# Start addresses of the large on-chip tiles moved to multiples of 512 bytes in an fp32 encoder layer

## The chip, the cores and the metric

The kernel runs on one core of one Trainium2 chip. The metric is the device time of one execution in microseconds (us). The kernel before took 1539.32 us (median of three runs, 1538.78 to 1539.38).

## The reference

One layer of an encoder over 1024 tokens of width 1024, all in float32, batch 1:

```
mod = silu(c) @ w_ada + b_ada                      -> sh1, sc1, gt1, sh2, sc2, gt2
h   = rms_norm(x, g_norm1) * (1 + sc1) + sh1
proj = h @ w_in                                    -> 8 heads of neighbourhood attention (qa, ka, va),
                                                      12 heads of dilated attention (qb, kb, vb), 2 x 1024 gates
o_a = softmax over an 8 x 16 window of a 16 x 64 grid, with a relative bias
o_b = three groups of 4 heads, dilations 1, 4, 16, merged by their log-denominators
merged = sigmoid(gate_a) * (o_a @ w_proj_a) + sigmoid(gate_b) * (o_b @ w_proj_b)
x   = x + gt1 * (merged @ w_o)
h2  = rms_norm(x, g_norm2) * (1 + sc2) + sh2
a, up = split(h2 @ w_ffn_in)                       (2 x 2816 columns)
x   = x + gt2 * ((silu(a) * up) @ w_ffn_out)
```

## The kernel before

**Precision.** Each large product is made of three matmuls. A float32 operand is split into `hi`, its rounding to the type `float32r`, and `lo = x - hi`, and the sum hi·hi + hi·lo + lo·hi is accumulated in PSUM (`PASS`, line 127). ScalarE makes `hi` (line 108), VectorE or GpSimd makes `lo` (line 109). A matmul has a stationary operand of 128 columns, loaded for it alone, and a moving operand of up to 512 columns, read from SBUF while it runs. Transposes, the row sums of line 263 and the product of probabilities and values (line 487) are plain float32.

**Stages**, in order of time in the profiled execution:

- 0 to 50 us: norm of x, modulation columns, the first unit's projection (lines 681 to 726).
- 50 to 600 us: ten units of two heads each. For each block of 128 tokens the projection (line 297: moving operand = weight tile `whi`/`wlo`, 384 columns; stationary = `hT`), transposes (355), scores (446), softmax, transposes of the probabilities (472), product with the values (487). Some gate products (604) follow at the end.
- 600 to 700 us: gate products by a scheme with seven instead of eight block products (623: moving = `hT` or the mixed blocks `tg`).
- 700 to 760 us: the two branch projections and the merge (995: moving = `oT`).
- 760 to 830 us: the output projection (1136: moving = kept weights `wr`, or `whi`/`wlo`).
- 830 to 1335 us: the first feed-forward product (1200: moving = `h2T`, or mixed blocks `t`; stationary = weights), again with seven products.
- 1335 to 1536 us: the second feed-forward product (1372: both operands are `whi`/`wlo` tiles), whose mixed weights `m` are loaded and formed at its start (lines 1343 to 1352).

**Order.** PE's order is the program's own (`manual_schedule`). Inside the first region the order of all engines is the program's; elsewhere a planner orders the other engines and the DMA queue by its own estimate. Nearly all DMAs are issued from SP.

**Where tiles lie.** SBUF is filled by two stacks of pools per partition, one growing up from the bottom (`left`), one growing down from the top (`right`). In a pool, tags are laid out in the order in which they are first allocated; each buffer is rounded up to 32 bytes. A pool that is opened after another was released lies on the same bytes, and a tile there waits for the last use of the tiles it covers (`reuse_waits="tile"`). At the very bottom lie 1024 bytes of DMA scratch and four constants of 32 bytes each. In the compiled program the starts of the large tiles, as remainders of 512 bytes, are:

| tiles | side | start mod 512 |
|---|---|---|
| `whi`, `wlo` (weight slots), `hT`, `h2T` (both parts), the `hi` halves of `tg`, `oT`, `t`, the tiles of the last stage `c11`.. and `x2` | left | 320 |
| the `lo` halves of `tg`, `oT`, `t`; `sg`, `wr`, `e`, `c`, `m`, `raw` | right | 480 |
| `yT`, `qk`, `land` and all of tag `big`, `PT`, `bmask`, `acc2` | right | 352 |
| `P`, `xd`, `stg` | right | 416 |
| `ident` | left | 448 |
| `xt` of the output projection, `tm`, `qn`, `rtab`, `gt1`, `sc2`, `sh2` | right | 0 |

All slices that matmuls take from these tiles begin at whole multiples of 512 bytes from the tile's start, but for the queries of the first unit, which begin 256 bytes on.

Of the kernel before, what the change touches and what calls it, by code (L numbers as in the profile page):

```python
# [10 lines left out]
F32 = mybir.dt.float32  # L11
# [20 lines left out]
LATE, NPRE = (3, 4, 5, 6, 7), 12  # L32
KFIRST, KLAST, OT = (3, 4, 2, 0, 5, 6, 1, 7), (2, 0, 1, 3, 4, 5, 6, 7), 3
PP, QT, AQ, AT, AV = 100, 0, 0, 0, 0
WARM = 40
XSQ = "avavaaaa"
XSC = "ddddvvvv"
# [4 lines left out]
def hybrid_layer(ctx: ExitStack, tc: tile.TileContext, x, colp, wada1, wada2, bada2, wqkv, wg, wpa, wpb,  # L42
# [3 lines left out]
    def pool(name, side, **kw):  # L46
        return tc.alloc_tile_pool(name=name, bufs=1, side=side, reuse_waits="tile", **kw)

    const = pool("const", "left")
    wp = pool("w", "left")  # L50
    rp = pool("raw", "right")
    ctx.enter_context(tc.manual_schedule(engines={mybir.EngineType.PE}))
# [11 lines left out]
    x2_d = tc.dram_tile([S, D], F32, name="x2_d")  # L64
    w1_d = tc.dram_tile([2, 4, 128, 512], F32, name="w1_d")
    e_d = tc.dram_tile([6, 2, 128, 512], F32, name="e_d")

    def bank(tag):
        return ps.tile([128, 512], F32, tag=tag, name="ps_" + tag)
# [22 lines left out]
    nc.vector.tensor_mul(cact, cact, c_c)  # L92
    bg1 = const.tile([128, 8], F32, name="bg1")
    nc.vector.scalar_tensor_tensor(bg1, bsc1, 1.0, g1_c, op0=ALU.add, op1=ALU.mult)

    def fview(ap):
        return ap.bitcast(F32)
# [6 lines left out]
    def wsplit(r, eng=None):  # L104
        n = r.shape[1]
        hi = wp.tile([128, 512], F32R, tag="hi", bufs=NHL, name="whi")
        lo = wp.tile([128, 512], F32R, tag="lo", bufs=NHL, name="wlo")
        nc.scalar.activation(hi[:, :n], r, AF.Copy)  # L108
        (eng or nc.gpsimd).tensor_sub(lo[:, :n], r, fview(hi[:, :n]))  # L109
        return hi, lo  # L110
# [26 lines left out]
    ap_ = pool("attn", "right")  # L137
# [7 lines left out]
    def big(name, shape=None, dtype=F32):  # L145
        return ap_.tile(shape or wide, dtype, tag="big", bufs=NBIG, name=name)

    yT = [ap_.tile([128, 4, S], F32, tag="qk", bufs=2, name="yT") for _ in range(2)]
    land = [big("land") for _ in range(NBIG)]
    seq = [0]  # L150

    def landing():
# [30 lines left out]
    pw = bank("t")  # L183
    for i in range(WARM):
        nc.tensor.transpose(pw[:, :128], ident, ident)
# [55 lines left out]
    rtab = []  # L241
# [8 lines left out]
                                        rg[:, qk, f, None, :].to_broadcast([128, 8, 16]), op=ALU.mult)  # L250
        return tb

    rg = const.tile([128, 2, 2, 16], F32, name="rg")
    nc.sync.dma_start(rg, ropeg)
    bm = ap_.tile([128, 512], F32, tag="bm", bufs=1, name="bmask")
    nc.sync.dma_start(bm, bmask)
# [361 lines left out]
    def gate_raw(i, q):  # L618
        return wload(wg[i, :, 4 * q:4 * q + 4, :], 512)
# [193 lines left out]
    for n in range(6, 92):  # L813
# [73 lines left out]
        if u < 10:  # L887
            proj_post(U, t)

    def gate_first(i, eng):  # L890
        for q, nm in enumerate(("w11", "w12")):
            gwt[i, nm] = wsplit(gate_raw(i, q), eng)
# [13 lines left out]
    for i in (3, 4):  # L906
        gate_first(i, None)
# [131 lines left out]
    def firsts(i):  # L1039
        for nm in ("w11", "w12"):  # L1040
            gate_prod(i, nm)

    gate_first(5, nc.vector)
    for i in (3, 4):
        firsts(i)
    gate_mixes(3, GORD)
    firsts(5)
    for i in (3, 4):
        gate_first(i + 3, nc.vector)
        for nm in GORD:  # L1050
            gate_prod(i, nm)
        gate_end(i)
        gate_mixes(i + 1, GORD)
        firsts(i + 3)
# [29 lines left out]
    wop = pool("wo", "right")  # L1084
# [12 lines left out]
    def o_post(t, pbs):  # L1097
        xt = wop.tile(wide, F32, tag="x", bufs=3, name="xt")
        nc.sync.dma_start(xt, x[t * 128:(t + 1) * 128, :])
        tm = tmp.tile(wide, F32, tag="tm", bufs=4, name="tm")  # L1100
        ss2 = wop.tile([128, 2], F32, tag="ss2", bufs=3, name="ss2")
        ss = wop.tile([128, 1], F32, tag="ss", bufs=3, name="ss")
        for hf in range(2):
            hs = slice(hf * 512, hf * 512 + 512)
            nc.vector.tensor_mul(tm[:, hs], pbs[hf], rows["gt1"][:, hs])
        for hf in range(2):
            hs = slice(hf * 512, hf * 512 + 512)
            nc.vector.tensor_add(xt[:, hs], xt[:, hs], tm[:, hs])
            nc.scalar.activation(tm[:, hs], xt[:, hs], AF.Square, accum_out=ss2[:, hf:hf + 1])
        nc.sync.dma_start(x2_d[t * 128:(t + 1) * 128, :], xt)  # L1110
        nc.vector.tensor_add(ss, ss2[:, 0:1], ss2[:, 1:2])
        r = rstd(wop, D, 1, ss, "x2")
        nc.vector.scalar_tensor_tensor(tm, xt, r, rows["sc2"], op0=ALU.mult, op1=ALU.mult)
        (nc.vector if t == 7 else nc.gpsimd).tensor_add(tm, tm, rows["sh2"])
        pend[t] = tm
# [14 lines left out]
    for t in range(8):  # L1130
# [8 lines left out]
                o_turn(t - 2)  # L1139
        o_post(t, pbs)  # L1140

    wj = {}

    gt = {}
# [288 lines left out]
    ps.release()  # L1433
    rp.release()
    wp.release()
    const.release()


# [98 lines left out]
```

## Time and profile before

| what | value |
|---|---|
| median of three runs | 1539.32 us |
| the profiled execution's own time | 1537.63 us |
| span of its instructions | 1535.8 us |
| PE busy (matmuls) | 1511.7 us, 8156 matmuls |
| VectorE, ScalarE, GpSimd busy | 1112.1, 669.3, 532.7 us |
| granted TensorE clock, mean | 0.999 |

Times in the profile are microseconds unless marked ns. PE stands for matmuls, PEld for the loads of stationary operands, which overlap them. Matmuls are pipelined: the duration of one is longer than the time after which the next begins, so the pace is read from start to start, or from the busy time of many in a row, not from the mean duration. 1.8 us of the execution's own time lie outside the span.

### The profile page before, as it was taken

How to read it: one execution, taken by the hardware profiler on the slowest of the kernel's cores; microseconds unless marked ns; L12 is line 12 of the kernel's file. 1: busy time of each engine (PE TensorE's matmuls, PEld its weight loads, DVE VectorE, ACT ScalarE, POOL GpSimd, SP SyncE). 2: the span in 40 equal slices, each digit the busy share in tenths (PEclk: the TensorE clock that was granted, in tenths of full speed). 3: DMA queues.
4: the chain of work that ended last, by engine and by line, in shares of the span. 5: the costliest groups of instructions: out<-in, count | busy, mean ns of one | idle time of the engine just before them, and what ended most of it. 6: DMA issues, size and time to landing. Idle time of an engine off the chain costs nothing. (4 is left out here: it accounts for less than half of the span.)

```text
span 1535.8 us, 24624 instructions
## 1 busy us (share of the span) xinstructions
PE 1511.7 (98%) x8156; PEld 1265.7 (82%) x8156; DVE 1112.1 (72%) x2428; ACT 669.3 (44%) x1719; POOL 532.7 (35%) x540
## 2 busy tenths in 40 slices
PE   8999999999999999999999999999999999999998
PEld 7988888898888877788888888888888888887886
DVE  6867687776889855466675497788767776599468
ACT  5555555655555453335542354232322333344442
POOL 0422331321000030001361221577767776104464
PEclk9999999999999999999999999999999999999999
DMA  9615355543354354843553235345443334798343
GB/s 368 227 50 169 114 158 168 184 159 88 98 148 135 103 169 139 285 145 117 171 163 140 81 105 178 114 140 171 152 134 105 104 110 137 242 375 286 104 151 103
DMA packets 158017, 241.67 MB, mean 157 GB/s; under 512 B 27313, under 2 KB 77361, under 8 KB 157121
## 3 DMA queue, kind: packets, MB, share of 16 engines
q1 hardware_dynamic: 156736, 235.90, 47.4%
q10 hardware_dynamic: 1152, 4.19, 0.7%
q8 instruction: 65, 1.06, 0.3%
q14 instruction: 64, 0.52, 0.1%
HBM read 179.89 MB, written 60.15 MB: 156 GB/s over the span
## 5 line engine op out<-in xcount | busy, mean ns | idle before, releaser
L109 POOL TENSOR_TENSOR wlo<-raw,whi 128x512 fp32r<-128x512 f32 (+2 forms) x133 | 170.5, 1294 | 473.0 <-ACT whi L108 453.8
L108 ACT ACTIVATE whi<-raw 128x512 fp32r<-128x512 f32 (+1 forms) x348 | 204.1, 600 | 284.0 <-DMA raw<-ga_d 33.7
L297 PE MATMUL ps_d<-whi,hT 128*128 128x384 f32 x1152 | 316.9, 343 | 1.4 <-ACT v L332 1.4
L109 DVE TENSOR_TENSOR wlo<-raw,whi 128x512 fp32r<-128x512 f32 (+1 forms) x215 | 183.0, 865 | 75.5 <-ACT whi L108 71.4
L297 PEld LDWEIGHTS ps_d<-whi,hT 128*128 128x128 f32 x1152 | 210.3, 188 | 7.0 <-ACT vs L335 2.6
L297 PE MATMUL ps_d<-wlo,hT 128*128 128x384 f32 x576 | 193.5, 336 | 0.4 <-POOL wlo L109 0.4
L297 PEld LDWEIGHTS ps_d<-wlo,hT 128*128 128x128 f32 x576 | 108.5, 188 | 0.7 <-POOL wlo L109 0.7
L108 ACT ACTIVATE whi<-ws 128x512 fp32r<-128x512 f32 x65 | 41.0, 630 | 127.6 <-DVE ws L1217 70.7
L1150 POOL TENSOR_TENSOR e<-e,c 128x512 f32<-128x512 f32 x44 | 68.6, 1558 | 65.3 <-DVE c L1280 40.3
L327 POOL TENSOR_TENSOR ra<-qn,rtab 128x64 f32<-128x64 f32 x48 | 16.7, 348 | 168.1 <-DVE qn L320 140.3
L461 ACT ACTIVATE P<-P,st 128x256 f32<-128x256 f32 (+2 forms) x100 | 46.1, 463 | 59.9 <-DVE st L460 59.9
L109 POOL TENSOR_TENSOR wlo<-m,whi 128x512 fp32r<-128x512 f32 x35 | 51.9, 1494 | 54.1 <-ACT whi L108 54.1
L604 PE MATMUL ps_d<-hT,whi 128*128 128x512 f32 x192 | 60.5, 396 | 0.0
L1200 PE MATMUL ps_v<-h2T,whi 128*128 128x512 f32 x192 | 59.6, 392 | 0.0
L1200 PE MATMUL ps_s<-h2T,whi 128*128 128x512 f32 x192 | 59.5, 391 | 0.0
L461 ACT ACTIVATE P<-P,sx 128x384 f32<-128x384 f32 (+1 forms) x64 | 37.1, 580 | 48.7 <-DVE sx L460 48.7
L1148 ACT ACTIVATE e<-e 128x512 f32<-128x512 f32 x44 | 27.4, 630 | 70.2 <-DVE e L1283 47.5
L1200 PE MATMUL ps_d<-h2T,whi 128*128 128x512 f32 x184 | 57.1, 392 | 0.0
L109 DVE TENSOR_TENSOR wlo<-ws,whi 128x512 fp32r<-128x512 f32 x45 | 50.9, 1130 | 8.0 <-ACT whi L108 8.0
L318 DVE TENSOR_REDUCE ss<-sq 128x4 f32<-128x256 f32 x80 | 33.1, 414 | 31.9 <-ACT sq L315 31.7
L487 PE MATMUL ps_v<-PT,v 128*64 128x128 f32 (+1 forms) x672 | 55.0, 284 | 1.0 <-DVE PT L476 1.0
L446 PE MATMUL ps_s<-qk 64*128 64x256 f32 (+3 forms) x492 | 53.9, 321 | 1.6 <-DVE st L460 1.2
(436 smaller groups left out, 3994.6 us busy)
## 6 DMA issues: line engine op xcount, KB each, us to landing
raw<-in_w_dram SPq DMA_DIRECT2D x139, 256.0 KB
ga_d<-e SPq DMA_DIRECT2D x77, 256.0 KB
raw<-ga_d SPq DMA_DIRECT2D x77, 256.0 KB
wa<-in_wada_dram SPq DMA_DIRECT2D x32, 512.0 KB
raw<-in_wqkv_dram SPq DMA_DIRECT2D x80, 192.0 KB
m<-in_w_dram SPq DMA_DIRECT2D x44, 256.0 KB
raw<-in_wg_dram SPq DMA_DIRECT2D x42, 256.0 KB
xt<-in_x_dram SPq DMA_DIRECT2D x16, 512.0 KB
```

What stands on the lines that cost most here:

```text
L108: nc.scalar.activation(hi[:, :n], r, AF.Copy)
L109: (eng or nc.gpsimd).tensor_sub(lo[:, :n], r, fview(hi[:, :n]))
L297: nc.tensor.matmul(pd[:, :384], tok(a, k, t), U.w[k][b][:, :384], start=(k == 0 and i == 0), stop=(k == KT - 1 and i == 2))
L318: nc.vector.tensor_reduce(ss, sq.rearrange("p (h d) -> p h d", h=4), axis=mybir.AxisListType.X, op=ALU.add)
L327: nc.gpsimd.tensor_tensor(v4(ra), v4(qn[:, :, 0:16]), tv(0, 0, 16), op=ALU.mult)
L446: nc.tensor.matmul(I.pS[h][:nq, :nk], U.qk[a][hs, I.q0:I.q0 + nq], U.qk[2 + b][hs, I.kb0 * 128:I.kb0 * 128 + nk], start=(i == 0), stop=(i ...
L461: nc.scalar.activation(P[:nq, :nk], P[:nq, :nk], AF.Exp, scale=-1.0, bias=nm, accum_out=sm)
L487: nc.tensor.matmul(po[hs, :nq], U.v[:, I.kb0 + i, hs], I.PT[h][:, i, :nq], start=(i == 0), stop=(i == nkb - 1))
L604: nc.tensor.matmul(st["p"], gw[i, br][j][a][:, kk * 128:(kk + 1) * 128], hT[b][:, k, hs], start=(k == 0 and q == 0), stop=(k == 7 and q == 2))
L1148: nc.scalar.activation(sg, a, AF.Sigmoid)
L1150: nc.gpsimd.tensor_mul(sg, sg, up)
L1200: nc.tensor.matmul(pb, w[p][:, k * 128:(k + 1) * 128], b[q][:, k], start=(k == 0 and i == 0), stop=(k == 3 and i == 2))
```

## The change

Tiles that nobody writes or reads are added: 480 bytes at the top of SBUF (`edge`), 192 bytes behind the constants, 384 bytes at the end of the attention pool, 32 bytes at the end of the pool of the output projection. In the attention pool ten tags are allocated once ahead of use (`place`), so that those with large buffers come first in its layout and the small ones behind them. The gain table `rg` is allocated ahead of the filler in its pool; its load stays where it was. With that, every tile of the table above, but for `ident`, begins at a multiple of 512 bytes. No instruction is added to the program text, and none is taken out.

```diff
+EDGE, CFILL, AFILL, OFILL = 480, 192, 384, 32
...
     const = pool("const", "left")
+    edge = pool("edge", "right")
+    edge.tile([128, EDGE // 4], F32, name="edge")
     wp = pool("w", "left")
     rp = pool("raw", "right")
...
+    def fill(p, n, name):
+
+        p.tile([128, n // 4], F32, name=name)
...
     nc.vector.scalar_tensor_tensor(bg1, bsc1, 1.0, g1_c, op0=ALU.add, op1=ALU.mult)
 
+    rg = const.tile([128, 2, 2, 16], F32, name="rg")
+    fill(const, CFILL, "cfill")
...
     land = [big("land") for _ in range(NBIG)]
+    for tag, n, bufs in (("bm", 512, 1), ("p", 384, 4), ("qn", 256, 5), ("rtab", 512, 1), ("acc2", 512, 1), ("pT", 384, 3),
+                         ("stg", 128, 3), ("vs", 128, 2), ("ra", 64, 2), ("rb", 64, 2)):
+        ap_.tile([128, n], F32, tag=tag, bufs=bufs, name="place")
     seq = [0]
...
-    rg = const.tile([128, 2, 2, 16], F32, name="rg")
     nc.sync.dma_start(rg, ropeg)
...
+    fill(ap_, AFILL, "afill")
+
     def gate_first(i, eng):
...
         o_post(t, pbs)
 
+    fill(wop, OFILL, "ofill")
     wj = {}
...
     wp.release()
+    edge.release()
     const.release()
```

## The prediction

> **What bounds the kernel now.** I read the page first, then the table of stretches of time.
>
> ```profile
> span 1535.8 us, 24624 instructions
> PE 1511.7 (98%) x8156; PEld 1265.7 (82%) x8156; DVE 1112.1 (72%) x2428; ACT 669.3 (44%) x1719; POOL 532.7 (35%) x540
> PEclk9999999999999999999999999999999999999999
> DMA  9615355543354354843553235345443334798343
> ...
> 300.00:600.00 300.00, 293.76 (x1988) 251.36 (x1988) 228.08 (x792) 155.28 (x531) 45.59 (x55) 1.00 0.45 135
> ...
> 900.00:1000.00 100.00, 100.00 (x443) 82.18 (x443) 79.28 (x120) 41.63 (x71) 28.77 (x22) 1.00 0.42 130
> ...
> 1345.00:1420.00 75.00, 73.27 (x319) 59.17 (x319) 71.25 (x102) 34.99 (x59) 16.93 (x11) 1.00 0.94 331
> ```
>
> In the stretches the columns after the length are PE, PEld, DVE, ACT and POOL (busy us and instructions), the clock, the share of the DMA engines and GB/s. PE is the bound: 1511.7 of 1535.8 us, at full clock, with VectorE next at 72%. In the feed-forward part (900 to 1000 us) PE has no hole at all. Only between 1345 and 1420 us do the DMA engines (0.94) and VectorE (71.25 of 75) stand beside it. So a tile's address matters if it changes the pace of matmuls, and I looked for that pace, in the chain of waits and in the list by time (start, length, count). First weight tiles against weight tiles, then the projection, both with every operand at 320 mod 512:
>
> ```profile
> 1443.46 1.36 PE ps_d L1372 x6
> 1444.82 1.36 PE ps_s L1372 x6
> ...
> 137.57 0.51 PE L297 MATMUL ps_d<-whi,hT 128*128 128x384 f32 x2
> 137.91 0.33 PE L297 MATMUL ps_d<-wlo,hT 128*128 128x384 f32 x1
> 138.09 0.51 PE L297 MATMUL ps_d<-whi,hT 128*128 128x384 f32 x2
> ```
>
> Six matmuls of 512 columns in 1.36 us are 226.7 ns each; three of 384 in 0.52 us (137.57 to 138.09) are 173.3. The difference, 53.4 ns for 128 columns, is the streaming itself: 213.3 ns for 512 and 160 for 384. **Each matmul thus pays 13.3 ns that don't depend on its length**, exactly 32 columns' worth. Now plain float32 matmuls:
>
> ```profile
> 134.46 0.60 PE L472 MATMUL ps_t<-ident,P 128*128 128x128 f32 x4
> 130.01 1.02 PE L263 MATMUL ps_t<-acc,ones 128*1 128x512 f32 x2
> ...
> L472 PE MATMUL ps_t<-ident,P 128*128 128x128 f32 x328 | 49.9, 275 | 2.3 <-DVE P L464 1.5 <-DVE rv L120 0.6 <-DVE oacc L572 0.2
> L263 PE MATMUL ps_t<-acc,ones 128*1 128x512 f32 x16 | 8.2, 590 | 0.6 <-DVE PT L476 0.6
> ```
>
> Taking the last one's duration off, the first group steps at (600 - 275) / 3 = 108 ns for 128 columns, the second at 1020 - 590 = 430 ns for 512. That is twice the streaming time (106.7 and 426.7) plus 2 to 3 ns. Where columns are read at half the rate, a new stationary operand and a new address cost 2 to 3 ns, not 13.3. Last, moving operands that start elsewhere:
>
> ```profile
> 825.71 3.68 PE L1136 MATMUL ps_v<-wr,h2T 128*128 128x512 f32 x15
> L1136 PE MATMUL ps_d<-wr,h2T 128*128 128x512 f32 x90 | 22.4, 398 | 0.0
> ...
> 738.34 0.63 PE L995 MATMUL ps_t<-oT,whi 128*128 128x512 f32 x2
> 739.03 0.62 PE L995 MATMUL ps_t<-oT,whi 128*128 128x512 f32 x2
> 739.73 0.63 PE L995 MATMUL ps_t<-oT,whi 128*128 128x512 f32 x2
> 740.43 0.40 PE L995 MATMUL ps_t<-oT,whi 128*128 128x512 f32 x1
> ```
>
> All moving tiles at 480 (`wr`): (3680 - 398) / 14 = 234.4 ns. Alternating 320 and 480 (`oT`): nine matmuls from 738.34 to 740.43, 232.2 ns. The streaming is the same 213.3. **So the start of the moving operand already sets part of the pace**: 226.7, 232, 234.
>
> **The change part by part.** It adds no instruction, DMA or wait. Fillers and `place` tiles have neither writer nor reader, and moving `rg`'s allocation moves no load; these cost 0. What it does is put every moving operand at 0 mod 512. Which matmuls that touches, from the stretch of the whole span for one line at a time, in the order 1200, 297, 1372, 623, 1136, 604, 995, 726 (PE and PEld busy, count):
>
> ```profile
> 0.00:1536.00 1536.00, 425.75 (x1848) 346.68 (x1848) 1.00 0.49 157
> 0.00:1536.00 1536.00, 333.35 (x1776) 306.11 (x1776) 1.00 0.49 157
> 0.00:1536.00 1536.00, 211.45 (x924) 172.82 (x924) 1.00 0.49 157
> 0.00:1536.00 1536.00, 96.92 (x420) 78.75 (x420) 1.00 0.49 157
> 0.00:1536.00 1536.00, 90.53 (x384) 71.78 (x384) 1.00 0.49 157
> 0.00:1536.00 1536.00, 69.14 (x288) 53.09 (x288) 1.00 0.49 157
> 0.00:1536.00 1536.00, 67.04 (x288) 53.99 (x288) 1.00 0.49 157
> 0.00:1536.00 1536.00, 27.18 (x144) 24.73 (x144) 1.00 0.49 157
> ```
>
> These are 4152 matmuls of 512 columns and 1920 of 384 (lines 297 and 726).
>
> *Step 1, unlike starts go.* Lines 1200, 623 and 995 hold 425.75 + 96.92 + 67.04 = 589.7 us for 2556 matmuls; at 226.7 ns they would be 579.4. Gain 10.3 us. The 240 with `wr` gain 240 x 7.7 ns = 1.8 us. Together **12 us**. That the best pace seen is kept at 0 is the part for which I have rows.
>
> *Step 2, the 13.3 ns themselves.* No row shows a moving operand of the full-rate kind at 0. The bounds: at best what the half-rate matmuls show is left, 2.3 ns, so 11 ns are gained; at worst a start at 0 is like the worst seen, 234.4, so 7.7 ns are lost. Between these I take the full 11 ns. The reason is the exactness: 226.7 and 173.3 ns are 17 and 13 times 13.33 ns, that is 17 and 13 blocks of 32 columns (128 bytes), for 16 and 12 blocks of data, and the 2 to 3 ns of the half-rate rows don't appear on top. A read that starts 64 bytes into such a block touches 17 and 13 of them; one that starts at its edge touches 16 and 12. Against it: a start at 480 touches 17 too and takes 234.4, so blocks of 128 bytes aren't the whole account. Gain 4152 x 11 = 45.7 us and 1920 x 11 = 21.1 us.
>
> The Trainium skill's page "TensorE: Matmul & The Clock Gate" (section "Wait — 56ns, not 53.3ns?") gives back-to-back matmuls N ÷ 2.4 GHz plus about 2.5 ns, measured for bf16, 215.7 ns at 512 columns; the trace's 226.7 is 11 above it, and by that rule the sum of step 2 would be the same.
>
> *Step 3, scores (line 446).* Their 492 matmuls run in pairs side by side, so at most 246 x 11 ns = 2.7 us; I take half, 1.3.
>
> *Step 4, what doesn't reach the end.* Between 1345 and 1420 us the DMAs need 0.94 x 75 = 70.5 us whatever PE does; PE's 319 x 11 ns = 3.5 us there count as lost. The 144 of line 726 lie in the first 50 us, where loads bound: 1.6 us lost. From 50 to 600 us PE waits here and there on the softmax chain; PE is 293.76 of 300 us busy there and VectorE 228.08, so I take off 15% of the projection's 1776 x 11 = 19.5 us, 3 us. Together 8 us. The rest passes whole: in the stretch from 900 us on VectorE has 79 us of work per 100, and PE's share would shrink to 95.
>
> *Step 5, other engines and DMAs.* Their starts move too; no row compares two starts for one operation. I take 0. Bounds: 0, and a gain of 4 us, if loads in the DMA-bound stretch went 6% faster, still behind PE's 70 us there.
>
> Sum: 12 + 45.7 + 21.1 + 1.3 - 8 = 72 us. From the execution's own 1537.6 us (span 1535.8 and 1.8 around it) that gives 1465.5; the median of the runs lies 1.7 above that execution, so **1467 us**.
>
> **The rivals.**
>
> *Only step 1 happens.* The 13.3 ns could belong to full-rate matmuls as such, for instance to the hand-over between their stationary operands, which no start changes. For it: 320 is a multiple of 64, and with blocks of 64 bytes the start at 480 costs just one block more (6.7 ns; 234.4 - 226.7 = 7.7), so that blocks of 64 and a fixed 32 columns account for all three paces. Against it: the fixed part is missing at half rate, where the operands are swapped just as often. Time: 1537.6 - 12 + 1.7 = 1527 us.
>
> *Half of step 2.* One block of 64 bytes is saved instead of one of 128, 6.7 ns: 6072 x 6.7 = 40.7, with step 1 and less 5 us of losses: 48, so 1491 us.
>
> *The start means nothing.* `wr` and the `lo` halves also lie on the right side, far from the rest, and that may be what slows them; the sides stay. Against it: `wr` alone, all of it on one side, has the slowest pace, without any change of side. Time 1539, within 0.2%. The Trainium skill's page "SBUF — State Buffer" (section "Door 1: The DMA port swizzle (why `[64,N]` ≈ `[32,N]`)") speaks for it: lines are 16 bytes there, and all starts before and after are multiples of 32, so none would gain. The trace's 234.4 against 226.7 doesn't fit that.
>
> *Slower: a start at 0 is a bad one.* All operands would start at the same place of a 512-byte row, and moving operand, stationary operand and the other engines' writes could meet in the same part of the memory. The price is the worst pace seen: 7.7 ns for the 4572 matmuls that now run at 226.7 or 173.3, and 2.2 ns for the 1260 mixed ones: 38 us, 1577. It decides from a mean pace above 230 ns on, against 425.75 / 1848 = 230.4 now in line 1200. Against it: with `whi` and `wlo`, all starts are equal already and the pace is the best of all.
>
> *Slower: the planner's order.* Another layout changes which old tiles a new one waits for, in the attention pool above all. A load that is held there costs PE one landing,
>
> ```profile
> 1363.01 5.37 DMA m<-in_w_dram
> ```
>
> 5 us, so 1544 if nothing else happens. Against it: the tiles that follow on the attention pool's bytes now cover the same or fewer old tiles, since `sg` and `big` buffers of 4096 bytes fall on the same edges.
>
> **How the numbers follow.** Full sum 0.50 (1455 to 1480 by itself, from the uncertainty of steps 4 and 5); half of step 2 0.07; step 1 alone 0.29; nothing 0.06; a bad start 0.05; the order 0.03. A measurement can tell 0.2% (3 us) from no change. Faster is the first three, 0.86; same 0.06; slower 0.08. The range reaches from 1455, the sum with its losses halved and the DMA's gain, to 1531, step 1 with a third of it missing; what lies outside is nothing, both slower cases and the tails, below 0.2.
>
> **What would show it.** Right: in the chain of waits of the last stage six matmuls take 1.29 to 1.30 us; in the projection three take 0.49; `t`, `oT` and `wr` have the same pace as the rest; the busy PE time of line 1200 falls from 425.75 to about 399 us. Step 1 alone: 1.36 us stays in the last stage, line 1200 falls to 419. Step 4 is right if the stretch of the `m` loads stays about 75 us long with holes in PE. The forecast is wrong if the pace of `whi` against `whi` doesn't move, or if it moves and PE then waits for VectorE in the units.

## The result: 0.75% faster, from one of the two gains that were counted

| | before | after |
|---|---|---|
| median of six runs each | 1538.51 us (1536.20 to 1539.38) | 1527.69 us (1523.93 to 1528.47) |
| the profiled execution's own time; span | 1537.63; 1535.8 us | 1527.74; 1526.0 us |

The ratio is 0.9925, with a 95% interval from 0.9912 to 0.9939: 10.8 us less, where 72 were forecast. Instructions that only wait set aside, all engines and the DMA queue have the same instructions in the same order in both compiled programs, so what differs is the pace.

The head of the page of after:

```profile
span 1526.0 us, 24623 instructions
PE 1501.5 (98%) x8156; PEld 1266.5 (83%) x8156; DVE 1110.0 (73%) x2428; ACT 666.4 (44%) x1719; POOL 534.1 (35%) x540
```

PE lost 10.2 us of busy time (1511.7 to 1501.5) and the span 9.8; VectorE, ScalarE and GpSimd moved by 1 to 3 us each and bound nothing. Where PE lost them is in the stretch of the whole span, one line at a time, for the same eight lines in the same order as before (now 1215, 309, 1387, 635, 1150, 616, 1009, 738; length, PE busy and count, PEld busy and count, clock, DMA share, GB/s):

```profile
0.00:1526.00 1526.00, 419.57 (x1848) 346.71 (x1848) 1.00 0.48 158
0.00:1526.00 1526.00, 332.78 (x1776) 305.56 (x1776) 1.00 0.48 158
0.00:1526.00 1526.00, 211.04 (x924) 172.97 (x924) 1.00 0.48 158
0.00:1526.00 1526.00, 95.67 (x420) 78.75 (x420) 1.00 0.48 158
0.00:1526.00 1526.00, 88.81 (x384) 71.63 (x384) 1.00 0.48 158
0.00:1526.00 1526.00, 69.14 (x288) 53.08 (x288) 1.00 0.48 158
0.00:1526.00 1526.00, 65.44 (x288) 54.05 (x288) 1.00 0.48 158
0.00:1526.00 1526.00, 27.10 (x144) 24.63 (x144) 1.00 0.48 158
```

The four lines that had operands with unlike starts fell: 6.18 us (`t`), 1.25 (`tg`), 1.72 (`wr`), 1.60 (`oT`), together 10.75. The other four, 3132 float32r matmuls, moved by 0.6 us or less. The list by time shows the paces (start, length, count): first the projection, then `oT`.

```profile
136.97 0.51 PE L309 MATMUL ps_d<-whi,hT 128*128 128x384 f32 x2
137.31 0.33 PE L309 MATMUL ps_d<-wlo,hT 128*128 128x384 f32 x1
137.49 0.51 PE L309 MATMUL ps_d<-whi,hT 128*128 128x384 f32 x2
...
738.51 0.61 PE L1009 MATMUL ps_t<-oT,whi 128*128 128x512 f32 x2
739.19 0.61 PE L1009 MATMUL ps_t<-oT,whi 128*128 128x512 f32 x2
739.87 0.61 PE L1009 MATMUL ps_t<-oT,whi 128*128 128x512 f32 x2
```

Three matmuls of 384 columns still take 0.52 us (136.97 to 137.49). Six of `oT` now take 1.36 us (738.51 to 739.87), 226.7 ns each, where it was 232.2. The chain of waits shows the last stage as it was, six matmuls in 1.36 us:

```profile
1433.62 1.36 PE ps_d L1387 x6
1434.98 1.36 PE ps_s L1387 x6
```

So the unlike starts went, and the pace that was already the best did not move. What PE waits for longest in after:

```profile
PE ps_s L458 <- DVE qk L388: 2.3, 1, 2.3
PE ps_t L576 <- ACT PT L490: 1.7, 1, 1.7
PE ps_d L1387 <- DVE wlo L119: 1.6, 3, 1.1
```

The first of these, a single wait in the units, was not among the longest before; in this one execution it gave back 2.3 us. In a second execution of the same kernel (run 6) it isn't among the longest either. The stretch with the `m` loads, moved by the 10 us that the span got shorter, is as full as before (PE 73.58 us where it was 73.27, DMA share 0.95):

```profile
1335.00:1410.00 75.00, 73.58 (x322) 59.94 (x321) 71.61 (x103) 34.90 (x59) 17.89 (x11) 1.00 0.95 337
```

### The profile page after: what moved, and what is told of

It reads as the page before. It is cut to its first block, busy times and chain, and to the rows that moved or that the text cites. A ratio compares the mean times of both kernels' runs of the same rounds, so it can differ in the third digit from the quotient of the medians.

```text
span 1526.0 us, 24623 instructions
## 1 busy us (share of the span) xinstructions
PE 1501.5 (98%) x8156; PEld 1266.5 (83%) x8156; DVE 1110.0 (73%) x2428; ACT 666.4 (44%) x1719; POOL 534.1 (35%) x540
## 4 chain that ended last, share of the span: by engine, by line
PE 81%; DVE 7%; DMA 6%; ACT 2%; issue 2%; POOL 1%; SPq 0%; DVEq 0%; POOLq 0%; ACTq 0%
PE ps_d L309 13%; PE ps_v L1215 7%; PE ps_d L1215 7%; PE ps_s L1215 7%; PE ps_t L1215 6%; PE ps_d L616 4%; PE ps_s L1387 3%; PE ps_d L1387 3%; PE ps_v L499 2%; PE ps_s L1150 2%; PE ps_d L1150 2%; PE ps_v L1387 2%; PE ps_s L458 2%; PE ps_t L1387 2%; PE ps_t L484 2%
## 5 line engine op out<-in xcount | busy, mean ns | idle before, releaser
L458 PEld LDWEIGHTS ps_s<-qk 64*128 64x128 f32 (+1 forms) x492 | 35.1, 182 | 25.7 <-issue 13.1
```

The costliest lines, as they stand in the source:

```text
L458: nc.tensor.matmul(I.pS[h][:nq, :nk], U.qk[a][hs, I.q0:I.q0 + nq], U.qk[2 + b][hs, I.kb0 * 128:I.kb0 * 128 + nk], start=(i == 0), stop=(i ...
```

## The experiments

Below, *distance* is the start of the moving operand less that of the stationary operand, modulo 256 bytes. Paces are means from start to start; in the blocks of runs 1 and 5 the first four steps are left out.

**1. The pace of one kind of matmul by itself.** A kernel that leaves the layer out and runs blocks of 49 matmuls without waits, the stationary slices six in turn. A block is given by its name, type, columns, the starts of its two moving tiles, the start of the stationary one, its columns and the PSUM banks:

```diff
+    ("same_aa", "r", 512, 0, 0, 0, 128, 1),
+    ("same_ab", "r", 512, 32, 32, 0, 128, 1),
...
+    ("stat_b", "r", 512, 0, 0, 32, 128, 1),
...
+            nc.tensor.matmul(pb[b][:w, :cols], t[2][:, s:s + w], t[q][:, o:o + cols],
+                             start=(i < nb), stop=(i >= N - nb))
```

> The computation is left out but for x copied to the output: 27 blocks of 49 matmuls that nothing holds up, one start of the moving operand or one kind of matmul per block, pace = (busy time of the block less the mean duration) / 48. Theory A (a moving float32r operand is read in blocks of 64 bytes, 6.7 ns each, and 32 columns' worth of time, 13.3 ns, are fixed): 226.7 ns for starts at 0, 64, 128, 256, 320 and for 0 mixed with 64; 233 to 235 for 32, 96, 224, 480; 173.3 at 384 columns. Theory B (blocks of 128 bytes, my forecast): 215.6 at 0, 128 and 256, 226.7 at 64 and 320. Theory C (unlike starts of two tiles in turn are what costs): every block with equal starts 226.7, those with mixed starts over 231. On the fixed part: if it is the hand-over of the stationary operand it shrinks with 64 and 32 stationary columns (220 and 217 instead of 226.7) or moves with the start of the stationary one; if it belongs to reading at full rate, it stays at 226.7 there and falls to 2 to 3 ns for bfloat16 (216) and plain float32 (429 per pass).

The stretch of the whole span, one block at a time (PE busy of 49 matmuls; in the last, plain float32, each of them is two passes), for float32r with moving and stationary starts 0 and 0, 32 and 0, 64 and 0, 256 and 0, 0 and 32; then bf16 with 0 and 0, bf16 with 32 and 0, plain float32 with 0 and 0:

```profile
0.00:364.00 364.00, 11.27 (x49) 9.20 (x49) 0.16 (x1) 1.00 0.07 26
0.00:364.00 364.00, 11.60 (x49) 9.18 (x49) 0.16 (x1) 1.00 0.07 26
0.00:364.00 364.00, 11.39 (x49) 9.20 (x49) 0.16 (x1) 1.00 0.07 26
0.00:364.00 364.00, 11.29 (x49) 9.20 (x49) 0.16 (x1) 1.00 0.07 26
0.00:364.00 364.00, 11.59 (x49) 9.20 (x49) 0.16 (x1) 1.00 0.07 26
0.00:364.00 364.00, 10.75 (x49) 0.16 (x1) 1.00 0.07 26
0.00:364.00 364.00, 10.74 (x49) 0.16 (x1) 1.00 0.07 26
0.00:364.00 364.00, 42.22 (x98) 18.54 (x98) 0.16 (x1) 1.00 0.07 26
```

Less the last matmul's duration (0.39 us) and over 48, the first is (11.27 - 0.39) / 48 = 226.7 ns; from start to start the eight are 226.66, 233.34, 228.98, 226.75, 233.34, 215.84, 215.84 and 429.16 ns. Two things follow. A start at 0 has no better pace than 226.7: the 11 ns that Step 2 wanted are not there to be had. And the fifth row is slow although its moving operand begins at 0: with the stationary operand moved by 32 bytes the pace is that of the moving operand moved by 32. It isn't the moving operand's own start that counts, so none of the three theories holds as written (A fails at 64, B at 0, and C at 32, where both moving tiles start alike). Moving starts of 320 and 480 against a stationary one at 0 have 228.8 and 233.3 ns, the paces of 64 and 224, which they are modulo 256. bf16 (whose rows show no separate loads) and plain float32 have the same pace at distances 0 and 32. A narrower stationary operand doesn't help (64 columns 230.1, 32 columns 231.6 ns at distance 0), and 384 columns take 173.3 ns at distance 0 and at 32.

The Trainium skill's rule in "TensorE: Matmul & The Clock Gate" (section "Wait — 56ns, not 53.3ns?"), N ÷ 2.4 GHz plus about 2.5 ns, gives 215.7 for 512 columns; bf16 measured 215.84 and agrees. float32r, at 226.7, doesn't follow it.

**2. One small tile at the top, nothing else.** The kernel before with 32 unused bytes at the top, so that the tiles on the right begin at 448 and those on the left stay at 320:

```diff
     const = pool("const", "left")
+    edge = pool("edge", "right")
+    edge.tile([128, 8], F32, name="edge")
...
+    edge.release()
```

> The kernel before with one unused tile of 32 bytes at the top of SBUF and nothing else: right-hand moving tiles start at 448 instead of 480 mod 512, those of the attention pool at 320 and 384, left-hand ones stay at 320; nothing large starts at 0. Theory A (multiples of 64 are enough): all of the change's gain, 1527 us, ratio 0.992 to 0.994, line of the first feed-forward product at 226.7 ns a matmul. Rival (the change needs 512, or equal starts of the two halves): 1538, ratio 1.000, 230 ns in that line.

Measured 1532.39 us (1530.46 to 1534.61), ratio 0.996 (0.9946 to 0.9974), between the two expectations. The line of the first feed-forward product (1202 here) in the whole span:

```profile
0.00:1540.00 1540.00, 421.38 (x1848) 346.60 (x1848) 1.00 0.49 157
```

Of the 6.18 us between before and after, 4.37 are gained. The matmuls with the `lo` half of `t` (distance 128) step at 234.2 ns and the two others of each three, with the `hi` half, at 226.7 and 225.8; before, both kinds were slow. So the right side's start against the left's decides, and 448, a multiple of 64, isn't enough.

**3. Everything at 32 instead of 0.** The changed kernel with the two outer fillers altered, so that all the large tiles begin at 32 mod 512:

```diff
-EDGE, CFILL, AFILL, OFILL = 480, 192, 384, 32
+EDGE, CFILL, AFILL, OFILL = 448, 224, 384, 32
```

> The changed kernel with its fillers set so that every large tile starts at 32 mod 512: all equal, none at a multiple of 64. Theory A: every full-rate matmul at 234 ns (181 for 384 columns), 6072 x 7.7 = 47 us above the changed kernel's 1527, so 1565 to 1577, ratio about 1.02. Theory C (unlike starts): 226.7 everywhere, 1527.

Measured 1530.57 us (1526.73 to 1532.69), ratio 0.9947 (0.9929 to 0.9965). The line of the first feed-forward product (1215):

```profile
0.00:1540.00 1540.00, 419.57 (x1848) 346.82 (x1848) 1.00 0.48 157
```

419.57 us, what it has with all starts at 0. Blocks of 64 bytes in absolute addresses are out: a start that halves such a block costs nothing if both operands have it. The total was 2.9 us above that of after, taken on another occasion; run 8 below has the two side by side.

**4. Only the left side moved.** The changed kernel with the right side back at 480; the left stays at 0, so the `lo` halves and `wr` are at distance 224:

```diff
-EDGE, CFILL, AFILL, OFILL = 480, 192, 384, 32
+EDGE, CFILL, AFILL, OFILL = 512, 192, 384, 32
```

> The changed kernel with 512 instead of 480 bytes at the top: the left stack at 0, the right one back at 480 mod 512. Theory A: the left side's part is worth nothing, all of the right-hand starts still cost, 1537 to 1540, ratio 1.000. Rival (each side gives a share): 1532 to 1534.

Measured 1535.26 us (1532.16 to 1536.87), ratio 0.9978 (0.9969 to 0.9987). Line 1215:

```profile
0.00:1540.00 1540.00, 423.15 (x1848) 346.95 (x1848) 1.00 0.48 157
```

Line 1215 keeps 3.58 us of its loss, and `wr` steps at 233.1 ns. The time lies between the two expectations. The stationary tiles and most moving ones lie at 0 mod 512 here, and only 3 us came of it; what changed for the slow matmuls is their distance, 224 where it was 160, and the four lines with `t`, `tg`, `wr` and `oT` gave 3.55 of their 10.75 us.

**5. All distances, and lengths.** Blocks as in run 1, with the stationary tile at 0 and the moving ones at every multiple of 16 below 256; other lengths; one stationary slice for all:

```diff
+    ("d016x", "r", 512, 16, 16, 0, 128, 1),
...
+    ("s00n504x", "r", 504, 0, 0, 0, 128, 1),
+    ("s32n504x", "r", 504, 32, 32, 0, 128, 1),
```

> The computation is left out but for x copied to the output: 34 blocks of 49 matmuls, as in the first run of this kind. The first blocks scan the distance from the start of the stationary operand (at 0) to that of the moving one in steps of 16 bytes up to 240. Theory D (the read of the next stationary operand meets the read of the moving one in the same part of SBUF, with a period of 256 bytes in their distance): 226.7 ns at 0, 229 at 64, 233.3 at 32, 96, 128, 224 as before, and, if the meeting can be avoided at all, one distance in between near 216. Theory E (a fixed 13.3 ns, with up to 6.7 more where the starts differ): nothing under 226.7 anywhere. Shorter moving operands (504 to 448 columns): by E columns x 0.417 + 13.3; by D steps that don't follow the length. With one stationary slice for all: as before in both, since it is loaded anew each time.

| distance | 0 | 16 | 32 | 48 | 64 | 80 | 96 | 112 |
|---|---|---|---|---|---|---|---|---|
| ns | 226.7 | 231.7 | 233.3 | 233.3 | 229.0 | 231.0 | 233.4 | 231.3 |
| **distance** | **128** | **144** | **160** | **176** | **192** | **208** | **224** | **240** |
| ns | 232.3 | 233.3 | 234.4 | 231.2 | 233.3 | 234.7 | 233.3 | 233.3 |

The blocks behind the best, the second best and the worst of these (distances 0, 64, 208) and, last, 504 columns at distance 0, in the stretch of the whole span:

```profile
0.00:373.00 373.00, 11.27 (x49) 9.20 (x49) 0.16 (x1) 1.00 0.07 26
0.00:373.00 373.00, 11.39 (x49) 9.21 (x49) 0.16 (x1) 1.00 0.07 26
0.00:373.00 373.00, 11.66 (x49) 9.23 (x49) 0.16 (x1) 1.00 0.07 26
0.00:373.00 373.00, 11.27 (x49) 9.20 (x49) 0.16 (x1) 1.00 0.07 26
```

Distance 0 has the best pace of the sixteen, 64 the next; the others are 4 to 8 ns above it. The distance of before, 160, is at 234.4, the pace of `wr`. So the bound of theory E holds at 512 columns, and theory D's distance near 216 ns is not among the sixteen. The length does not add up as "columns plus 32", which was E's sum. Nor do all lengths care for the distance (ns; 384 columns are from run 1):

| columns | 512 | 504 | 496 | 480 | 448 | 384 | 256 | 128 |
|---|---|---|---|---|---|---|---|---|
| distance 0 | 226.7 | 226.7 | 223.3 | 216.7 | 202.6 | 173.3 | 120.0 | 111.7 |
| distance 32 | 233.3 | 226.7 | 224.5 | 217.8 | 206.7 | 173.3 | 116.7 | 111.7 |

The blocks of 256 columns, first at distance 0, then at 32:

```profile
0.00:373.00 373.00, 6.04 (x49) 6.01 (x49) 0.16 (x1) 1.00 0.07 26
0.00:373.00 373.00, 5.88 (x49) 5.86 (x49) 0.16 (x1) 1.00 0.07 26
```

The whole 6.7 ns are lost at 512 columns alone: 504 and 384 lose nothing, and 256 columns are 3.3 ns faster at distance 32 than at 0. With one stationary slice for all matmuls the pace is 227.2 at distance 0 and 233.3 at 128, so it isn't a matter of which slice is loaded.

The Trainium skill's page "SBUF — State Buffer" (section "Door 1: The DMA port swizzle (why `[64,N]` ≈ `[32,N]`)") has lines of 16 bytes. A distance of exactly one such line costs 5.0 ns (231.7 against 226.7), so whole lines aren't what has to match here.

**6. After, once more.** The changed kernel unaltered, beside the next two:

> The changed kernel once more, beside the two runs below on the same chip: 1527 to 1529 us, ratio 0.992 to 0.994.

Measured 1525.19 us (1522.38 to 1529.43), ratio 0.992 (0.9905 to 0.9935), a little under the expected time.

**7. 256 against 512.** The changed kernel with the right side at 256 mod 512, the left at 0:

```diff
-EDGE, CFILL, AFILL, OFILL = 480, 192, 384, 32
+EDGE, CFILL, AFILL, OFILL = 224, 192, 384, 32
```

> The changed kernel with 224 instead of 480 bytes at the top: left stack at 0, right stack at 256 mod 512. Theory D (distance of moving and stationary starts modulo 256): the same pace as the changed kernel, 226.7 ns in all lines, the same time within 2 us. Rival (modulo 512): 231 to 234 ns where the moving tile lies on the right (lo halves, kept weights), 1533 to 1536.

Measured 1525.33 us (1523.82 to 1527.29), ratio 0.9919 (0.9906 to 0.9932); line 1215:

```profile
0.00:1540.00 1540.00, 419.57 (x1848) 346.81 (x1848) 1.00 0.48 157
```

The same pace as with everything at 0: the distance counts modulo 256, as run 1 had it for the matmuls alone.

**8. All at 32, once more.** The kernel of run 3 beside run 6:

> All large tiles at 32 mod 512 once more, beside the changed kernel. Theory D: same pace, so the same time as the changed kernel within 2 us. Rival (multiples of 64 or 512 are worth something to the other engines or the DMAs): 3 us slower, as the first runs of the two, on different occasions, had it.

Measured 1527.36 us (1524.31 to 1531.08), ratio 0.9933 (0.9919 to 0.9948), line 1215 at 419.57 us again. That is 2.2 us above run 6, at the edge of what the expectation allowed and on the same side as the 2.9 us of run 3. The intervals overlap, and line 1215 has the same pace; whether a start at 32 costs something elsewhere is neither shown nor excluded.

**9. The smallest change that makes all distances 0.** The kernel before with 160 unused bytes at the top and nothing else. The right side then begins at 320, as the left always did; no filler behind the constants or in a pool, the attention pool in its old order, and the operands of the large products at no multiple of 512, nor of 128:

```diff
     const = pool("const", "left")
+    edge = pool("edge", "right")
+    edge.tile([128, 40], F32, name="edge")
...
+    edge.release()
```

> The kernel before with one unused tile of 160 bytes at the top of SBUF and nothing else: right-hand tiles that move against left-hand stationary ones start at 320 mod 512 as these do, so the distance of every such pair is 0 mod 256; no start is a multiple of 128, and the attention pool keeps its order. Theory D: the changed kernel's pace in all lines (226.7 ns) and its time, 1524 to 1528 us, ratio 0.991 to 0.994. Rival (the fillers behind the constants and in the two pools, or multiples of 512, are worth something by themselves): between 1528 and 1538.

Measured 1526.04 us (1524.91 to 1533.57), ratio 0.9918 (0.9905 to 0.993). Lines 1202 and 1138 (`wr`) in the profiled execution, the slowest of seven:

```profile
0.00:1540.00 1540.00, 419.60 (x1848) 346.70 (x1848) 1.00 0.48 157
0.00:1540.00 1540.00, 89.15 (x384) 71.56 (x384) 1.00 0.48 157
```

That is the whole gain of the change. Its other parts (multiples of 512, the fillers, the `place` tiles) brought nothing that these runs can measure.

**10. Which read stalls.** Blocks as in run 1 with three matmuls in turn, each with a PSUM tile of its own (a, b, c); in b the moving operand is 128 bytes further on (`mv`), or the stationary one (`st`), or both; `next` has the moving one of b and the stationary one of c further on; `mw`, `sw`, `bothw` and `nextw` are the same four with 32 bytes. A block is given by the starts of the moving operand in a, b and c, then those of the stationary one:

```diff
+    ("mv", (0, 128, 0), (0, 0, 0)),
+    ("st", (0, 0, 0), (0, 128, 0)),
+    ("both", (0, 128, 0), (0, 128, 0)),
+    ("next", (0, 128, 0), (0, 0, 128)),
+    ("mw", (0, 32, 0), (0, 0, 0)),
...
```

> The computation is left out but for x copied to the output: ten blocks of 48 matmuls of 512 columns in three turns a, b, c, in which the start of the moving operand, of the stationary one, or of both is shifted by 128 (then by 32) bytes in one turn. Theory D1 (a moving operand meets the load of the following stationary one, which runs beside it): with the moving operand shifted in b it is b that is slow; with the stationary one shifted in b, a is slow; with the moving one shifted in b and the stationary one in c, none is. Theory D2 (it meets its own stationary operand's place): with the stationary one shifted in b, b is slow; with both shifted in b, none is.

A step runs from a matmul's start to that of the next (ns):

| block | step of a | of b | of c |
|---|---|---|---|
| `plain` | 227 | 226 | 227 |
| `mv` | 226.7 | 234.3 | 225.7 |
| `st` | 232.7 | 234.0 | 226.7 |
| `both` | 229.2 | 231.0 | 233.5 |
| `next` | 232.7 | 229.0 | 231.7 |
| `mw` | 233.0 | 235.0 | 232.0 |
| `sw` | 239.1 | 229.0 | 231.9 |
| `bothw` | 231.0 | 232.5 | 232.3 |
| `nextw` | 233.6 | 231.9 | 231.9 |

The groups of `st` show the same in the durations (mean of one in ns, behind the comma; undisturbed is 389):

```profile
L54 PE MATMUL st_b<-rta,rtc 128*128 128x512 f32 x16 | 6.4, 397 | 0.0
L54 PE MATMUL st_a<-rta,rtc 128*128 128x512 f32 x16 | 6.3, 396 | 0.0
...
L54 PE MATMUL st_c<-rta,rtc 128*128 128x512 f32 x16 | 6.2, 389 | 0.0
```

If a matmul met only its own stationary operand, `both` would have no slow step; if it met only the one loaded for the matmul behind it, `next` would have none. Neither is so. In `st` a moved stationary operand slows its own matmul and the one ahead of it, during which it is loaded; `both` and `next` don't follow from that either. In `mw` one moving operand in three is 32 bytes off, and all three steps are slow: their mean, 233.3 ns, is that of a block in which every one is off (run 1). The two simple accounts fall, and none takes their place.

## Why the prediction was right and wrong

**Step 1, "unlike starts go", is right.** It put 10.3 us on three lines and 1.8 on `wr`; they gave 6.18 + 1.25 + 1.60 = 9.03 and 1.72. The difference of 1.3 us on the three lines is there mostly because 226.7 ns times the count leaves out what a line's busy time also holds: the last matmul of each group that something else follows counts with its whole duration (1.0 us). The step's words were too short, though: it compared moving operands among themselves. Runs 1, 2 and 4 show that a moving operand is to be compared with the stationary one. In before, the left side's operands and the stationary tiles began at 320 (distance 0), and the `lo` halves and `wr` at 480 (distance 160). Run 5 has 226.7 and 234.4 ns at these two distances, the paces of `whi` against `whi` and of `wr`. The third, 232.2 for `oT`, lies above the mean of two matmuls at distance 0 and one at 160 (229.3 ns); the last section takes this up.

**Step 2, "the 13.3 ns themselves", is where the forecast failed.** It counted 45.7 + 21.1 us and the runs gave none: no start tried has float32r at 512 columns under 226.66 ns (runs 1 and 5), and 384 columns stay at 173.3. So the fixed 13.3 ns, which the step took for a matter of the start, remain at every start tried. Three things were wrong in its working.

- 17 and 13 blocks of 13.3 ns fit a fixed 32 columns just as well as a block half used at its ends. The exactness could not choose between the two, and the working took it as choosing.
- The row that spoke against it, `wr` at 480, which touches 17 blocks too and took 234.4 ns, was named and set aside. Nor could the rows of before tell the moving operand's start from its distance to the stationary one, since the stationary tiles of all these products begin at 320; run 1 could.
- The lower bound was taken from plain float32 matmuls, whose two rows give 1.7 and 3.3 ns on top of the streaming. Run 1 has these at 429.16 ns per pass and bf16 at 215.84, both at distances 0 and 32: what float32r pays on top at distance 0 belongs to that kind of matmul, not to where its operand lies.

**Steps 3 and 4** hang on step 2 and went with it: nothing was saved on the scores (53.93 us busy before, 54.12 after), and of the 8 us of losses none was due, since the matmuls of line 738, of the projection and of the `m` stretch had nothing to lose. **Step 5**, nothing on the other engines and the DMAs, holds: VectorE 1112.1 to 1110.0 us busy, the DMA share in the `m` stretch 0.94 to 0.95.

**The rivals.** *Only step 1 happens* had the time (1527 against 1527.69) and both signs that it named, 1.36 us per six in the last stage and 419 us for the busiest line (419.57). Half of its reason fell: blocks of 64 bytes would have made run 3 as slow as before or slower. The other half, a fixed part that no start changes, stands for the 512 and 384 columns of this kernel. *Half of step 2* needed 220 ns and is out by the same paces. *The start means nothing* blamed the side: in run 9 all tiles stay on their sides, and the loss is gone. *A start at 0 is a bad one* is out by the rows of after, and *the planner's order* by the order, which is the same. The prediction gave *only step 1* 0.29 and the full sum 0.50; by its own rows it should have been the other way round, since step 1 was made of paces that had been seen, and step 2 of one that hadn't. That the time lies inside the stated range (1455 to 1531) it owes to this rival, not to the sum.

**Two things stay open:** which of PE's reads holds up which (run 10), and what the time of 32 columns at distance 0 is for. It is exact at 256, 384 and 512 columns (120.0, 173.3 and 226.7 ns), about 3 ns more at 448 to 504, and far more at 128 (111.7). Why 256 columns are faster at distance 32 is open with it.

## What to carry to other kernels

In a kernel of float32r matmuls of 512 columns, give the tiles that are multiplied with each other equal starts modulo 256 bytes; one unused tile at the edge of a stack did it here (160 bytes, 12 us). For shorter ones measure first: at 384 columns distance 32 cost nothing, and at 256 it was the better one. Look for it in the steps from start to start, class by class, with the starts of both operands beside each. A pace better than any in the trace has to be measured by itself before it is counted: here two blocks of 49 matmuls, of 512 and of 384 columns, would have settled 67 of the 72 us.

## What was not expected of the hardware

**The two operands of a float32r matmul aren't independent in time.** The Trainium skill's page "TensorE: Matmul & The Clock Gate" (section "Step-by-step: what each phase is for") says that the array reads its moving operand and loads its next weights through two independent read ports, and that the one takes no bandwidth from the other. Run 1 doesn't fit that for float32r at 512 columns: with the moving operand untouched, 32 bytes more in the stationary operand's start cost 6.7 ns of each step (226.66 to 233.34), and the measurement decides here. Whether it is read bandwidth that is lost, or something else that the two share, no run shows.

**A slow step is handed on.** The list by time of before, twice the same kind of product from `h2T`, with all operands at 320; the first follows another such product, the second one with `t`:

```profile
936.32 0.61 PE L1200 MATMUL ps_s<-h2T,whi 128*128 128x512 f32 x2
937.00 0.61 PE L1200 MATMUL ps_s<-h2T,whi 128*128 128x512 f32 x2
...
1005.29 0.63 PE L1200 MATMUL ps_v<-h2T,whi 128*128 128x512 f32 x2
1005.99 0.63 PE L1200 MATMUL ps_v<-h2T,whi 128*128 128x512 f32 x2
```

Three matmuls take 0.68 us in the first and 0.70 in the second. Over all start times of line 1200 (154 products of twelve matmuls), the 66 mixed products lose 4.5 us against 226.67 ns a step, and the 44 equal products that follow one lose 1.7 us, all of it in their first eight steps: together the 6.2 us of the row. In runs 2 and 4 (distances 128 and 224) the mixed products lose 1.8 and 3.5 us and those behind them nothing. So at distance 160 the loss also depends on what ran up to eight matmuls earlier, which may be why `oT` was slower than the mean of its two distances, and why the turns of run 10 fit no account that looks at neighbours alone.
